# Rows of the expert weights w1 and w3 laid two to a partition, in a one-layer decoder kernel on Trainium2

## The chip, the cores and the metric

The kernel runs on one core of a Trainium2 chip. The metric is the device time of one execution in microseconds. Three runs of the kernel before took 893.99, 894.02 and 895.39 us; their median is 894.02 us.

## What is computed

One layer of a decoder: two token mixers, a cross-attention and a mixture of experts, each with a residual and a layer norm. The change touches the experts alone. There are 512 tokens of 1024 values and 16 experts; each token goes to two of them.

```
for e in range(N_EXPERTS):
    hidden = jax.nn.silu(hf @ w1[e]) * (hf @ w3[e])
    y = y + combine[:, e:e + 1] * (hidden @ w2[e])
```

w1[e] and w3[e] are 1024 x 512 in float32 (2 MB each), w2[e] is 512 x 1024 (2 MB). All 16 experts together are 96 MB, read from HBM once.

## The kernel before

The mixers and the cross-attention run first, up to about 594 us. The experts follow in a pipeline over e = 0 to 15, written out by hand.

**Weights.** The class `Weights` holds one list of all weight pieces of the program, each of 512 KB, in the order of their use. `load` issues one DMA on the SyncE queue (SPq in the profile, line 54) whenever a buffer is free. A buffer comes back when `done` is called for its piece, after the last matmul on it. The buffers are named raws, ring, ringout, xres, sbk and s; there are some forty of them in the expert stage. The order of the expert pieces is: eight of w1 and w3 of expert e (w1 and w3 in turn, `q_up[e]`), then four of w2 of expert e - 1 (`q_w2[e - 1]`). A piece of w1 or w3 is 256 rows of 512 values. Partition p of the buffer holds rows p and 128 + p of the piece, so each partition receives two runs of 2 KB from two places. A piece of w2 is 128 rows of 1024 values: partition p holds row p, one run of 4 KB.

A load waits for two things (its rows of the order below name them): for PE, which must be done with the buffer, and for one of eight counters DMAHW0 to DMAHW7. The counters are used in turn, so a load waits until the load eight places ahead of it has landed, and at most eight loads are on their way.

**Tokens.** Tokens of an expert are gathered from DRAM by `gather` (POOL, line 1158) into `ringgb` or `wx`, one token in a partition. `turn_in` (lines 1390 to 1397) turns them with eight TensorE transposes of 128 columns (line 1395) into `xgT[:, e % 2, c]`, c = 0 to 7: 128 of the 1024 values in the partitions, the tokens in the columns. In a transpose the tokens are the operand that is loaded as weights, and the identity is streamed.

**Expert.** `up(e)` multiplies chunk c of the turned tokens with chunk c of w1 and w3 (line 1422; the parts for more than 64 and more than 96 tokens, line 1433, are skipped by a branch, line 1409 or 1411, where the expert has fewer). So the values that sit in partition p of `xgT[:, c]` must belong to the weight row that sits in partition p of chunk c. Then `turn_in(e + 1)`, `gather(e + 3)`, `down(e - 1)` with w2 (lines 1463 and 1471), `to_rows` (ACT line 1486 and 1492, DVE line 1494), and `scatter` (POOL, line 1270), which adds the result rows to `yd` in DRAM.

**The end.** After the loop `last_loads` (lines 1524 to 1540) reads `yd` back with four loads of 512 KB on SPq (line 1530). They stand on SPq behind all weight loads, behind the end of a block that is built by `tc.If(n > 0)` (line 1264; the block itself is not executed), and they need the scatter of expert 13 and all earlier ones. ACT and DVE split the rows read (lines 190 and 191). Behind those splits in the order of the two engines stand the copies of the last expert's turned hidden values (lines 1586 and 1588), and PE's last w2 matmuls (line 1595) wait for those copies.

Line 495, in an earlier stage, matters as a comparison. Its streamed operand is read with this pattern, m being 1, 2, 4, 8, 16, 32 and 64 in turn:

```
qt = strided(Q[:, h, 2 * c * P:], n * g + m, [[P - m, 2], [2 * m, n // (2 * m)], [1, m]])
```

With m = 1 (the group I-776 of the profile) these are two runs of 16 columns, every second one; with m = 16 (I-1162) two runs of 16 neighbouring columns.

Of the kernel before, what the change touches and what calls it, by code (L numbers as in the profile page):

```python
# [16 lines left out]
P = 128  # L17
# [79 lines left out]
def tile_kernel(ctx, tc, x, mem, ln_in_g, ln_in_b, w_in, hg_lb_logits, hg_norm_g, w_branch_a, w_branch_b,  # L97
                w_mix_out, ln1_g, ln1_b, xa_wq, xa_wk, xa_wv, xa_wo, ln2_g, ln2_b,
                router_wg, router_bg, router_we, router_be, moe_w1, moe_w3, moe_w2, ln3_g, ln3_b, out):
    nc = tc.nc  # L100
# [8 lines left out]
    W = Weights(nc, 2)  # L109

    def block(w, c0, nk):

        return [W.add(w[2 * q * P:(2 * q + 2) * P, c0:c0 + 512].rearrange("(k p) n -> p k n", p=P))
                for q in range(nk // 2)]
# [9 lines left out]
    q_v.append(block(xa_wv, 512, 8))  # L124
    q_wo = [block(xa_wo, c, 8) for c in (0, 512)]

    q_up, q_w2 = {}, {}
    for e in range(17):
        if e < 16:
            q_up[e] = [tuple(W.add(w[0, e, 2 * q * P:(2 * q + 2) * P].rearrange("(k p) n -> p k n", p=P), True)  # L130
                             for w in (moe_w1, moe_w3)) for q in range(4)]
        if e > 0:
            q_w2[e - 1] = [W.add(moe_w2[0, e - 1, k * P:(k + 1) * P].rearrange("(k p) n -> p k n", p=P), True)
                           for k in range(4)]
# [5 lines left out]
    def msp():  # L140
        return ps.tile([P, 512], F32, tag="ms", name=nc.get_next_instruction_name() + "_ms")
# [34 lines left out]
    ident = pp.tile([P, P], F32, name="ident")  # L176
# [225 lines left out]
    for lv in range(5):  # L402
        n = 32 >> lv
# [36 lines left out]
    for lv in range(1, 8):  # L440
        n = 2048 >> lv
# [768 lines left out]
    t = NT - 1  # L1210
# [176 lines left out]
    gx = [wx.rearrange("p a n -> p (a n)"), gbr[:, 1]]  # L1387
    scratch = []

    def turn_in(e):  # L1390
        xg = gx[e % 2]
        for q in range(2):
            p = msp()
            for i in range(4):
                nc.tensor.transpose(p[:, i * P:(i + 1) * P], xg[:, (4 * q + i) * P:(4 * q + i + 1) * P], ident)  # L1395
            (nc.scalar.copy, nc.vector.tensor_copy)[q](xgT[:, e % 2, 4 * q:4 * q + 4],
                                                       p.rearrange("p (k n) -> p k n", n=P))

# [98 lines left out]
    for e in range(NE - 1):  # L1497
        h = up(e)
        turn_in(e + 1)
        if e + 3 < NE:  # L1500
            gather(e + 3)
        if e == 13:
            scratch.extend(W.raw_free.pop() for i in range(4))
            more_blocks()
            W.buffers(scratch)
        if e == 0:
            begin(tell_gates())
        if e > 0:
            for step in down(e - 1):
                step()  # L1510
            finish()
            scatter(to_rows(e - 1), gidx[:, e - 1:e])
        turn_hidden(e, h)
# [68 lines left out]
    p = msp()  # L1582
# [109 lines left out]
```

## Time and profile before

| What | Value |
|---|---|
| Median of three runs | 894.02 us |
| Profiled execution: its own time | 894.34 us |
| Span of the profile (first to last instruction) | 892.4 us |
| Mean granted TensorE clock | 0.989 of full speed |
| PE busy | 845.3 us, 95% of the span |
| DVE, ACT, POOL busy | 51%, 38%, 14% |
| SyncE queue (q1) | 157.31 MB in 71504 packets |
| All DMA | 177.65 MB, mean 199 GB/s |

The profiled execution is 0.32 us above the median of the three runs, and its span leaves out 1.94 us of its own time. Times of the rows below count from the start of the span. A line number of the profile is a line of the kernel above. "PEld" is the load of the operand that stays in TensorE, which overlaps the matmuls; "PEq" and "SPq" are the sequencers of PE and SyncE. In a row of the timeline the part in brackets is how long the engine was idle before it, and what ended that.

### The profile page before, as it was taken

What the parts mean: (1) busy time and instruction counts of PE and PEld (TensorE: products, weight loads), DVE (VectorE), ACT (ScalarE), POOL (GpSimd) and SP (SyncE); (2) the same over time, 40 slices, a digit from 0 to 9 for tenths busy, and PEclk for the clock granted to TensorE, in tenths of its full rate; (3) what the DMA queues carried; (4) which work ended last, traced back from release to release, by engine and by line L of the source; (5) the groups of instructions that cost most, each with busy time, mean ns of one, the idle gap of its engine ahead of it and who ended that gap; (6) DMA issues with size and microseconds to landing.
All of it is one profiled execution on the core that took longest, in us unless ns stands there. A gap on an engine that the chain in (4) does not pass through costs nothing. (4 is left out here: it accounts for less than half of the span.)

```text
span 892.4 us, 13680 instructions
## 1 busy us (share of the span) xinstructions
PE 845.3 (95%) x5296; PEld 582.1 (65%) x5296; DVE 458.6 (51%) x804; ACT 337.4 (38%) x640; POOL 128.4 (14%) x214
## 2 busy tenths in 40 slices
PE   7999999999999999999999999997999999799984
PEld 5888777788777777888988888763333333244343
DVE  6632576643757656759734667673423233223236
ACT  3332335643554544303624443222323233222234
POOL 5300000000312220005100000220211112110102
PEclk8999999999999999999999999999999999999998
DMA  8533323213222245422841766799999999999942
GB/s 298 174 98 95 95 73 94 71 49 95 71 71 72 71 139 177 140 88 80 239 158 48 235 214 236 250 372 343 390 353 356 333 343 339 342 366 360 370 170 94
DMA packets 79267, 177.65 MB, mean 199 GB/s; under 512 B 7797, under 2 KB 7829, under 8 KB 79184
## 3 DMA queue, kind: packets, MB, share of 16 engines
q1 hardware_dynamic: 71504, 157.31, 50.5%
q0 software_dynamic: 7536, 18.65, 6.7%
q8 instruction: 60, 0.98, 0.4%
q10 hardware_dynamic: 144, 0.52, 0.1%
q14 instruction: 23, 0.19, 0.1%
HBM read 168.47 MB, written 15.73 MB: 206 GB/s over the span
## 5 line engine op out<-in xcount | busy, mean ns | idle before, releaser
L1494 DVE TENSOR_SCALAR ringgb<-I-5389_acc,wgb 32x256 f32<-32x256 f32 x60 | 29.2, 487 | 122.5 <-ACT ringgb L1492 111.1
L1422 PE MATMUL I-5383_acc<-ring,xgT 128*64 128x512 f32 x284 | 77.9, 596 | 2.9 <-DMA ring<-in_moe_w_dram 2.9
L1486 ACT ACTIVATE ringgb<-I-5387_acc,wgb 64x512 f32<-64x512 f32 x30 | 20.5, 683 | 83.5 <-DMA yd<-ringgb,s 56.0
L67 DVE TENSOR_TENSOR I-69_out<-raws,I-69_out 128x1024 fp32r<-128x1024 f32 x24 | 29.3, 1223 | 38.2 <-ACT I-69_out L65 37.9
L1422 PEld LDWEIGHTS I-5383_acc<-ring,xgT 128*64 128x64 f32 x284 | 23.2, 137 | 36.9 <-issue 31.2
L1270 POOL DMA_INDIRECT yd<-ringgb,s x14 | 22.4, 1597 | 169.5 <-DVE I-8217w2k L1452 18.0
L660 DVE TENSOR_TENSOR_SCAN wx<-sbk 128x128 f32<-128x128 f32 (+3 forms) x32 | 27.1, 847 | 28.7 <-POOL sbk L656 28.7
L65 ACT CAST I-73_out<-raws 128x1024 fp32r<-128x1024 f32 x23 | 24.1, 1050 | 45.5 <-PE I-3563_acc L187 17.1
L67 DVE TENSOR_TENSOR I-71_out<-raws,I-71_out 128x1024 fp32r<-128x1024 f32 x22 | 26.9, 1223 | 24.6 <-ACT I-71_out L65 24.6
L65 ACT CAST I-69_out<-raws 128x1024 fp32r<-128x1024 f32 x25 | 26.2, 1050 | 32.6 <-issue 9.2
L65 ACT CAST I-71_out<-raws 128x1024 fp32r<-128x1024 f32 x24 | 25.3, 1055 | 24.9 <-PE I-384_acc L186 4.6
L67 DVE TENSOR_TENSOR I-73_out<-raws,I-73_out 128x1024 fp32r<-128x1024 f32 x21 | 25.7, 1222 | 16.1 <-ACT I-73_out L65 15.8
L1422 PE MATMUL I-5383_acc<-raws,xgT 128*64 128x512 f32 x64 | 30.0, 602 | 0.6 <-DMA raws<-in_moe_w_dram 0.6
L1492 ACT ACTIVATE ringgb<-I-5389_acc,wgb 32x256 f32<-32x256 f32 x60 | 27.8, 464 | 4.3 <-issue 2.2
L656 POOL TENSOR_SCALAR_AFFINE_SELECT sbk<-sbk 128x128 f32<-128x128 f32 x32 | 14.3, 447 | 94.5 <-ACT sbk L651 50.2
L1433 PE MATMUL I-5385_acc<-ring,xgT 128*32 128x256 f32 x408 | 26.4, 380 | 0.0
L1433 PEld LDWEIGHTS I-5385_acc<-ring,xgT 128*32 128x32 f32 x408 | 14.1, 110 | 13.8 <-issue 4.9
L213 POOL TENSOR_TENSOR I-1461hgss<-I-1461hgss,mhalf 128x4 f32<-128x4 f32 x1 | 1.0, 1047 | 136.4 <-DVE I-1461hgss L564 136.4
L1422 PE MATMUL I-5383_acc<-ringout,xgT 128*64 128x512 f32 x80 | 17.9, 595 | 0.0
L937 POOL MEMSET I-4802w2k<- 128x128 f32 x1 | 0.2, 204 | 110.0 <-PE I-4748_ms L187 110.0
L1422 PEld LDWEIGHTS I-5383_acc<-raws,xgT 128*64 128x64 f32 x64 | 8.1, 138 | 8.6 <-issue 7.0
L1158 POOL DMA_INDIRECT ringgb<-x2d,s x8 | 8.4, 1048 | 29.0 <-PE I-7818_ms L1395 9.8
(3489 smaller groups left out, 2397.3 us busy)
## 6 DMA issues: line engine op xcount, KB each, us to landing
ring<-in_moe_w_dram SPq DMA_DIRECT2D x114, 512.0 KB
raws<-in_w_in_dram SPq DMA_DIRECT2D x44, 512.0 KB
ringout<-in_moe_w_dram SPq DMA_DIRECT2D x32, 512.0 KB
raws<-in_moe_w_dram SPq DMA_DIRECT2D x20, 512.0 KB
xres<-in_moe_w_dram SPq DMA_DIRECT2D x16, 512.0 KB
raws<-in_xa_wk_dram SPq DMA_DIRECT2D x7, 512.0 KB
raws<-in_xa_wv_dram SPq DMA_DIRECT2D x7, 512.0 KB
raws<-in_w_mix_out_dram SPq DMA_DIRECT2D x6, 512.0 KB
```

Of the source, the lines that this page charges most:

```text
L65: self.nc.scalar.copy(hi, raw)
L67: eng.tensor_tensor(lo, raw, hi.bitcast(F32), op=ALU.subtract)
L213: nc.gpsimd.tensor_tensor(o, v, mhalf[:, :v.shape[-1]], op=ALU.pow)
L656: nc.gpsimd.affine_select(kp[:, d], kp[:, d], pattern=[[-1, P]], compare_op=ALU.is_gt, fill=1.0, base=w * (P - 1), channel_multiplier=1 - ...
L660: nc.vector.tensor_tensor_scan(rest[:, :n][:, ::-1], kp[:, n:0:-1], kp[:, n:0:-1], 1.0, ALU.mult, ALU.bypass)
L1158: nc.gpsimd.indirect_dma_start(out=gx[e % 2], out_offset=None, in_=x2d[:, :], in_offset=bass.IndirectOffsetOnAxis(ap=gidx[:, e:e + 1], axi ...
L1270: nc.gpsimd.indirect_dma_start(out=yd[:, :], out_offset=bass.IndirectOffsetOnAxis(ap=idx, axis=0), in_=y, in_offset=None, bounds_check=T - ...
L1422: nc.tensor.matmul(a[64 * i:64 * i + 64], x[:, c, 0:64], w[:, k * 512:(k + 1) * 512], start=c == 0, stop=c == 7)
L1433: nc.tensor.matmul(b[32 * i:32 * i + 32, 256 * g:256 * g + 256], x[:, c, 64 + 32 * g:96 + 32 * g], ws[c // 2][i // 2][:, o:o + 256], start ...
L1486: nc.scalar.activation(y[0:64, n * 512:(n + 1) * 512], a[s], AF.Copy, scale=gates_at[s, 0, e:e + 1])
L1492: nc.scalar.activation(o, z, AF.Copy, scale=f)
L1494: nc.vector.tensor_scalar(o, z, f, None, op0=ALU.mult)
```

## The change

Two places change. The pieces of w1 and w3 of experts 1 to 15 are read so that partition p of the buffer holds rows 2p and 2p + 1 of the piece: one run of 4 KB, as in w2. Expert 0 keeps its layout, because its tokens come another way (they are gathered by matmuls, not by `turn_in`). And `turn_in` takes, for chunk c = 2q + k, every second column of the 256 columns of piece q, from column k on, so that tokens and weight rows fit again. The buffers, the matmuls of `up`, the copies out of PSUM and the number of bytes stay as they are.

```
-            q_up[e] = [tuple(W.add(w[0, e, 2 * q * P:(2 * q + 2) * P].rearrange("(k p) n -> p k n", p=P), True)
+            q_up[e] = [tuple(W.add(w[0, e, 2 * q * P:(2 * q + 2) * P].rearrange("(k p) n -> p k n", p=P) if e == 0 else
+                                   w[0, e, 2 * q * P:(2 * q + 2) * P].rearrange("(p k) n -> p (k n)", k=2)[:, None], True)
                              for w in (moe_w1, moe_w3)) for q in range(4)]
...
     def turn_in(e):
-        xg = gx[e % 2]
+        xg = gx[e % 2].rearrange("t (q p k) -> t q k p", q=4, k=2)
         for q in range(2):
             p = msp()
             for i in range(4):
-                nc.tensor.transpose(p[:, i * P:(i + 1) * P], xg[:, (4 * q + i) * P:(4 * q + i + 1) * P], ident)
+                nc.tensor.transpose(p[:, i * P:(i + 1) * P], xg[:, 2 * q + i // 2, i % 2], ident)
```

No instruction moves on any engine and none is added or removed; after the first place, line numbers are three higher. On SPq, at the last four of expert 15's loads of w1 and w3 and the first three of expert 14's loads of w2 (the buffer stands left of the arrow), the order before is:

```order
L54 DMA ring4_4376<-in_moe_w1_dram 128x2x512 [waits DMAHW7_49,PE_49]
L54 DMA ring11_4717<-in_moe_w3_dram 128x2x512 [waits DMAHW0_49,PE_49]
L54 DMA ring11_4717<-in_moe_w1_dram 128x2x512 [waits DMAHW1_49,PE_49]
L54 DMA ring12_4720<-in_moe_w3_dram 128x2x512 [waits DMAHW2_49,PE_49]
L54 DMA ring12_4720<-in_moe_w2_dram 128x1024 [waits DMAHW3_49,PE_49]
L54 DMA ring6_4723<-in_moe_w2_dram 128x1024 [waits DMAHW4_49,PE_49]
L54 DMA ring6_4723<-in_moe_w2_dram 128x1024 [waits DMAHW5_49,PE_49]
```

and with the change:

```order
L54 DMA ring4_4376<-in_moe_w1_dram 128x1024 [waits DMAHW7_49,PE_49]
L54 DMA ring11_4717<-in_moe_w3_dram 128x1024 [waits DMAHW0_49,PE_49]
L54 DMA ring11_4717<-in_moe_w1_dram 128x1024 [waits DMAHW1_49,PE_49]
L54 DMA ring12_4720<-in_moe_w3_dram 128x1024 [waits DMAHW2_49,PE_49]
L54 DMA ring12_4720<-in_moe_w2_dram 128x1024 [waits DMAHW3_49,PE_49]
L54 DMA ring6_4723<-in_moe_w2_dram 128x1024 [waits DMAHW4_49,PE_49]
L54 DMA ring6_4723<-in_moe_w2_dram 128x1024 [waits DMAHW5_49,PE_49]
```

The loads of w1 and w3 have the shape of the w2 loads now; buffers, places and waits are the same. On PE, at the end of expert 2's `up` and at `turn_in(3)` (tokens in ringgb), the order before is:

```order
L1433 MATMUL I-5385_acc<-ring_5044,xgT 32x256 x8
L1411 UNCONDITIONAL_BRANCH x2
L1409 UNCONDITIONAL_BRANCH
L1395 MATMUL I-5911_ms<-ident,ringgb 128x128 x4
L1395 MATMUL I-5918_ms<-ident,ringgb 128x128 x4
L1463 MATMUL I-5387_acc<-ring_5138,I-5803w2k 64x512 x4
```

and with the change:

```order
L1436 MATMUL I-5385_acc<-ring_5044,xgT 32x256 x8
L1414 UNCONDITIONAL_BRANCH x2
L1412 UNCONDITIONAL_BRANCH
L1398 MATMUL I-5911_ms<-ident,ringgb 128x128 x4
L1398 MATMUL I-5918_ms<-ident,ringgb 128x128 x4
L1466 MATMUL I-5387_acc<-ring_5138,I-5803w2k 64x512 x4
```

Only the line numbers differ; that the transposes read every second column does not show in such a row.

## Rows read from the trace of the kernel before

**Rows 1.** The page, part 2: tenths busy in 40 slices of 22.3 us.

```profile
PE   7999999999999999999999999997999999799984
...
DMA  8533323213222245422841766799999999999942
```

**Rows 2.** By stretch: PE, PEld, DVE, ACT, POOL busy, PEclk, DMA share, GB/s.

```profile
760.00:780.00 20.00, 13.35 (x55) 4.76 (x52) 4.70 (x8) 5.55 (x10) 2.64 (x2) 0.91 0.98 351
842.50:846.00 3.50, 3.50 (x20) 1.22 (x18) 1.97 (x4) 0.00 (x0) 1.41 (x2) 1.00 1.02 407
846.00:850.00 4.00, 4.00 (x54) 1.75 (x53) 1.56 (x3) 0.59 (x1) 0.74 (x2) 1.00 0.67 204
640.00:840.00 200.00, 182.68 (x1342) 73.29 (x1338) 56.44 (x96) 59.56 (x108) 29.62 (x22) 0.99 0.99 353
```

**Rows 3.** Waits of PE, 755 to 790 us: total, times, longest.

```profile
PE I-5383_acc L1422 <- DMA ring<-in_moe_w_dram: 2.9, 3, 1.5
PE I-5383_acc L1422 <- DMA s<-in_moe_w_dram: 0.7, 1, 0.7
PE I-5383_acc L1422 <- DMA raws<-in_moe_w_dram: 0.6, 1, 0.6
```

**Rows 4.** Timeline of PE, two groups of line L1463: start, length.

```profile
692.57 3.65 PE L1463 MATMUL I-5387_acc<-ringout,I-6563w2k 128*64 128x512 f32 x16
...
774.38 4.97 PE L1463 MATMUL I-5387_acc<-ring,I-7513w2k 128*64 128x512 f32 x15 [3.14 <-issue]
```

**Rows 5.** Timeline of the DMA queue SPq, 800 to 862 us.

```profile
807.49 0.60 SPq L54 DMA_DIRECT2D ring<-in_moe_w_dram  x1
808.77 4.34 SPq L54 DMA_DIRECT2D raws<-in_moe_w_dram  x2
...
839.72 0.33 SPq L54 DMA_DIRECT2D s<-in_moe_w_dram  x1
841.05 1.65 SPq L54 DMA_DIRECT2D ring<-in_moe_w_dram  x2
855.57 1.77 SPq L1530 DMA_DIRECT2D ringout<-yd  x4
```

**Rows 6.** Line L1264, SPq: ns of one, first and last start.

```profile
L1264 SPq EVENT_SEMAPHORE  x9: 17/17/17, 844.1 to 855.2; - x9
```

**Rows 7.** The chain that ended last, in order of time.

```profile
856.06 4.44 DMA ringout<-yd
...
861.66 1.24 DVE zp L191
```

**Rows 8.** Timeline of all engines, 838 to 866 us.

```profile
844.59 1.56 POOL L1270 DMA_INDIRECT yd<-ringgb,s  x1 [16.79 <-DVE I-8392w2k L1452]
...
858.89 1.93 PE L1471 MATMUL I-5389_acc<-ring,I-8392w2k 128*32 128x256 f32 x32
...
863.70 1.12 PE L1595 MATMUL I-5383_acc<-ring,I-8529w2k 128*128 128x512 f32 x2 [2.87 <-ACT I-8529w2k L1588]
```

**Rows 9.** DMA issues, scatter of results: count, median us to landing.

```profile
yd<-ringgb,s POOLq DMA_INDIRECT x14, 9.0
```

**Rows 10.** DMA queue, 522 to 535 us, runs of 2 KB: packets, MB, share.

```profile
q1 hardware_dynamic: 2169, 4.18, 88.6%
```

**Rows 11.** DMA queue, 842.5 to 846 us, runs of 4 KB.

```profile
q1 hardware_dynamic: 391, 1.43, 101.8%
```

**Rows 12.** DMA queue, 640 to 840 us, both kinds.

```profile
q1 hardware_dynamic: 27954, 64.14, 86.4%
```

**Rows 13.** Line L1395, four weight loads: min/median/max ns, first and last start.

```profile
L1395 PEld LDWEIGHTS I-5685_ms<-ident,wx x4: 137/140/143, 617.0 to 617.3; 128*128 128x128 f32 x4
```

**Rows 14.** Line L495, m = 1 (I-776) and m = 16 (I-1162).

```profile
L495 PE MATMUL I-776_ms<-hgQ,wx x64: 191/196/218, 99.4 to 101.6; 128*32 128x32 f32 x64
...
L495 PE MATMUL I-1162_ms<-hgQ,wx x64: 196/196/217, 137.3 to 139.6; 128*32 128x32 f32 x64
```

**Rows 15.** Timeline of PE, the wait for the first gathered tokens.

```profile
606.74 1.11 PE L1395 MATMUL I-5542_ms<-ident,ringgb 128*128 128x128 f32 x4 [4.00 <-DMA ringgb<-x2d,s]
```

## Prediction

> **What bounds the kernel now.** I read the page's slices first. PE is at 9 tenths in nearly every slice, and from about 580 us on the DMA engines are at 9 tenths too, until about 850 us [rows 1]. So the expert stage is the one place where bytes can be the limit, and the change touches only that stage. Over 640 to 840 us the DMA share is 0.99 at 353 GB/s, while PE has a matmul in flight for 182.7 of 200 us [rows 2]. Two engines that are both nearly full say little on which one is waited for, so I went to the waits.
>
> PE starves in one stretch. Between 755 and 790 us its waits for pieces of w1 and w3 are 2.9, 0.7 and 0.6 us, together 4.2 us [rows 3]. In the same stretch the granted clock is 0.91 [rows 2], and one group of 15 matmuls of line 1463 takes 4.97 us, where 16 took 3.65 us at the full clock [rows 4]. That is 4.97 - 15/16 x 3.65 = 1.5 us lost at the lower level (1.2 GHz) after those idle times. The 3.14 us before that group [rows 4] have no releaser in the profile; I leave them where they are.
>
> The second place is the end. The chain that ended last starts on SPq: the first reads of yd are issued at 855.57 us [rows 5], they take 4.44 us, and the split of the rows read and the two copies behind it follow [rows 7]. PE's last w2 matmuls start at 863.70 us after 2.87 us of idle time for those copies [rows 8]; PE had been done at 858.89 + 1.93 = 860.82 us. Why does SPq issue at 855.57 and not earlier? Its last weight load was issued soon after 841.05 us [rows 5]. Then it stands at line 1264 and goes through nine waits, the first at 844.1, the last at 855.2 us [rows 6]. Nothing of PE is waited for there. These are the eight DMA counters, that is, the landing of the last weight loads. In 846 to 850 us the DMA share is only 0.67 [rows 2]: some of the 16 engines are still draining their part while others are done. So **the end of the kernel hangs on the end of the weight stream**, and PE only has to be there in time.
>
> **What the change removes.** Each load of w1 or w3 becomes 128 runs of 4 KB instead of 256 of 2 KB; per DMA engine 8 packets instead of 16. What is that worth? The trace has both kinds.
> - In 522 to 535 us the queue carries only w1 and w3: 0.886 x 16 x 13 us = 184.3 us for 4.18 MB / 2048 = 2041 packets, 90 ns each [rows 10].
> - In 842.5 to 846 us it carries only w2: 1.018 x 16 x 3.5 us = 57.0 us for 1.43 MB / 4096 = 349 packets, 163 ns each [rows 11].
> - So one load costs an engine 16 x 90.3 = 1.445 us in the one form and 8 x 163.3 = 1.307 us in the other: 0.14 us less.
> - Over 640 to 840 us both kinds are mixed, two thirds of the bytes in 2 KB runs by the order of the list: 2764.8 us for 20879 and 5220 packets [rows 12]. With 90.3 ns for the small ones, 168 ns are left for a large one, and the difference is 1.445 - 1.348 = 0.10 us a load.
> - The strictest row is the pace of SPq near the end. A load is issued when the one eight places ahead has landed. The loads at 807.49 and 808.77 us follow the landing of two w2 loads, 1.28 us apart; those at 839.72 and 841.05 us follow two loads of expert 15's w1 and w3, 1.33 us apart [rows 5]. That is 0.05 us a load.
>
> The ends are 0.05 and 0.14 us. I take 0.07 us, nearer to the pace, because the pace is set by the engine that lands last, and that engine also sets the end.
>
> How many loads count? The first forty or so only need the buffers to be there, and their successors wait for PE, which begins at about 594 us. I count experts 5 to 15: 88 loads; from expert 6 it is 80, from 4 it is 96. The weight stream then ends 88 x 0.07 = **6.2 us** earlier.
>
> **What that moves.** At the end, the nine waits of line 1264 end at 855.2 - 6.2 = 849.0 us. What is late next? The reads of yd also need the scatter of expert 13: issued at 844.59 us [rows 8], 9.0 us to landing by the median [rows 9], so 853.6 us, 1.6 us before the weights. It moves only as far as PE and the two engines behind it move. By expert 12, 64 loads have given 64 x 0.07 = 4.5 us, which is enough for the 4.2 us of waits; with those gone the 1.5 us at the lower clock may go too, but the loads don't allow more than 4.5. So the scatter lands at about 849.1 us, and SPq is free 6.1 us earlier. PE is done at 860.8 - 4.5 = 856.3 us and could be called from 863.7 - 6.1 = 857.6 us on, so it still waits there for 1.3 us. Behind that the program is the same. The sum is a gain of 6.1 us.
>
> **What it adds.** No instruction. The 120 transposes of `turn_in` (8 for each of experts 1 to 15) load their weights from every second column. One group of four starts its weight loads within 617.0 to 617.3 us, 140 ns each, about 0.11 us apart [rows 13]. No row shows a weight load with a step. The nearest rows are streamed operands: 64 matmuls with every second column take a median of 196 ns, and with neighbouring columns 196 ns too [rows 14]. So I take nothing, with a bound of nothing below (it reads no fewer columns) and a doubling above, 8 x 0.11 = 0.9 us an expert, which the first rival prices. The Trainium skill's page "SBUF — State Buffer" (section "Door 1: The DMA port swizzle") says that an engine reading with a step keeps its full rate while at least two accesses fall into one 16-byte line; two float32 of four do here. No run here shows it for weight loads.
>
> The gathers share the DMA engines with the weights. PE waits 4.00 us for the first gathered tokens [rows 15]. An engine has eight rows of a gather; if each lets one weight packet pass, which is now 163 instead of 90 ns, the wait grows by 0.6 us. PE's 1.3 us at the end hide it from PE, but the scatter of expert 13 moves by it. I take nothing and keep 0.6 us as the bound.
>
> **The rivals.**
> - **Slower: the stepped weight loads cost.** At a doubling PE has 15 x 0.88 = 13.2 us more to do, on its own path in the experts where the weights are there in time. It has 4.2 + 1.5 + 2.9 = 8.6 us of idle and slow time to pay with, so the kernel loses 4.6 us: **898.6 us**. It decides from 8.6 us / 120 = 72 ns a transpose on. For it: there is no such load in the trace. Against it: [rows 14].
> - **No change: the bytes bind, not the packets.** Then loads of either form take the same time beside each other, and the time stays at **894.0 us**. For it: the pace differs by only 0.05 us, and at 353 GB/s [rows 2] the memory itself could be the limit. Against it: 407 GB/s with 4 KB packets alone [rows 2]. The Trainium skill's page "DMA: Bandwidth & Descriptors" (section Specifications) speaks for this rival: runs of 512 B already reach the line rate, and one core's share of HBM is about 358 GB/s. By that rule the gain is nothing. The stretch at 407 GB/s is above that share.
> - **Half of it:** the stream ends earlier, but the scatter of expert 13 or a gather does not follow, because PE gains little. A scatter that moves by 1.5 us only lets SPq go 3.1 us earlier: **890.9 us**.
> - **More:** with 0.10 us and more a load the stream no longer binds; PE's 8.6 us and the 3.1 us without a releaser go too: **about 883 us**.
>
> **How the numbers follow.** The profiled execution took 894.34 us, 0.32 above the median of the runs. 894.3 - 6.1 = 888.2 us, and 0.3 less against the median: 887.9 us. The forecast's own range runs from 80 x 0.05 = 4.0 us (890.0) to the 8.6 us that PE can give up (885.4). A measurement of this kernel can tell about 0.2%, 1.8 us, from no change. Chances: the forecast 0.53, half of it 0.09, more 0.06, no change 0.18, slower 0.14. Faster is 0.53 + 0.09 + 0.06 = 0.68. For 8 in 10 the range leaves out the slower rival (0.14) and the lower part of "more" (0.03): 884.5 to 895.0 us.
>
> **What would show it.** In the profile after: the queue's packets fall by 15 x 8 x 128 = 15360; the waits for w1 and w3 at 755 to 790 us are gone or under 1 us, and the clock there stays at 1.00; the last wait of line 1264 on SPq is at about 849 us; the transposes still take 140 ns. Wrong would be: longer weight loads at line 1398 (the slower rival), or waits of SPq that end where they did (no change), or an end of line 1264 that moved while the reads of yd wait for the scatter (half).

## The result, and the profile after

The changed kernel takes **889.95 us** (median of 8 runs, 887.37 to 893.52). The kernel before took 895.04 us beside it (8 runs, 893.99 to 896.91). The medians differ by 5.1 us; the ratio of the comparison is 0.9924, with a 95% interval of 0.9903 to 0.9944, which is 0.56 to 0.97% faster. In a later comparison, on one chip, it was 890.23 against 896.13 us, 0.9937 (0.9914 to 0.9960). The medians thus differ by 5.1 and 5.9 us, and the two intervals together allow 4 to 9 us; 6.1 had been forecast, from 894.02 us. From the 895.04 us of this comparison the same 6.1 would have given 888.9.

The changed kernel's profiled run took 890.44 us, its span is 888.3 us. The packets of SPq's queue fell from 71504 to 56144, by 15360:

```profile
q1 hardware_dynamic: 56144, 157.31, 49.4%
```

The page's slices, 22.2 us each, answer [rows 1]: the rows look much the same, so the change hardly shows at this distance.

```profile
PE   6999999999999999999999999998989999889994
...
DMA  8433232223212225331852567599999999999942
```

The stretches (PE, PEld, DVE, ACT, POOL busy, PEclk, DMA share, GB/s) answer [rows 2]:

```profile
760.00:780.00 20.00, 17.26 (x82) 6.63 (x80) 4.70 (x8) 5.58 (x10) 2.64 (x2) 1.00 1.00 362
840.00:846.00 6.00, 6.00 (x32) 1.82 (x32) 3.52 (x7) 0.30 (x1) 2.15 (x2) 1.00 0.74 267
846.00:850.00 4.00, 4.00 (x76) 2.40 (x80) 0.68 (x1) 0.59 (x1) 0.00 (x0) 1.00 0.36 77
640.00:840.00 200.00, 185.22 (x1358) 76.45 (x1354) 56.42 (x96) 62.66 (x114) 29.61 (x22) 1.00 0.99 360
```

Over 640 to 840 us the DMA engines are as full as before, 0.99, but they move 360 GB/s instead of 353. PE is busy for 2.5 us more of the 200. At 760 to 780 us the granted clock is 1.00, the upper level, where it was 0.91. Between 755 and 790 us PE still waits for two pieces of w1 and w3, 2.3 us in place of 4.2 [rows 3]:

```profile
PE I-5383_acc L1425 <- DMA ring<-in_moe_w_dram: 1.8, 1, 1.8
PE I-5383_acc L1425 <- DMA s<-in_moe_w_dram: 0.5, 1, 0.5
```

The timeline of PE has the group of line 1466 that answers the slow one of [rows 4]. It takes 3.65 us, as the other group of [rows 4] did, and the idle time without a releaser ahead of it is 1.59 us instead of 3.14:

```profile
772.47 3.65 PE L1466 MATMUL I-5387_acc<-ring,I-7513w2k 128*64 128x512 f32 x15 [1.59 <-issue]
```

The end, in the order of [rows 5] to [rows 8]. First SPq's last loads and the reads of yd (timeline: start, length):

```profile
806.10 1.61 SPq L54 DMA_DIRECT2D raws<-in_moe_w_dram  x2
...
837.50 1.60 SPq L54 DMA_DIRECT2D ring<-in_moe_w_dram  x2
851.41 1.78 SPq L1533 DMA_DIRECT2D ringout<-yd  x4
```

The nine waits of line 1267 (ns of one, first and last start):

```profile
L1267 SPq EVENT_SEMAPHORE  x9: 17/17/17, 840.5 to 851.0; - x9
```

The first pieces of the chain that ended last (start, length):

```profile
859.19 0.43 issue
859.61 3.67 PE I-5383_acc L1598 x8
```

And the timeline of PE's last groups, with the copy on ACT that the last one needs:

```profile
857.12 1.93 PE L1474 MATMUL I-5389_acc<-ring,I-8392w2k 128*32 128x256 f32 x32
858.82 0.27 ACT L1591 COPY I-8529w2k<-I-8523_ms 128x128 f32<-128x128 f32 x1 [1.75 <-DVE I-8529w2k L1589]
859.61 1.10 PE L1598 MATMUL I-5383_acc<-ring,I-8529w2k 128*128 128x512 f32 x2 [0.56 <-PEq L1414]
```

Here the change is plain. The last loads are issued from 837.50 us on instead of 841.05. The nine waits end at 851.0 us instead of 855.2, the reads of yd go out at 851.41 instead of 855.57. And the chain no longer begins at SPq: behind line 1474 (done at 857.12 + 1.93 = 859.05 us) PE stands for 0.56 us for its own sequencer, where it waited 2.87 us for the split rows before [rows 8]. The copy is done at 858.82 + 0.27 = 859.09 us, so PE and the chain from SPq now end within 0.1 us of each other, and what is left is PE's own. In a second profile of the changed kernel the copy is done 1.1 us ahead of PE.

**A ruler for the experiments.** The expert stage does not start at one time: its first matmul of w1 stands at 594.9 us before and at 596.2 after, though nothing ahead of it was changed, and in a second profile of the changed kernel at 598.0. This row of the changed kernel shows the start (after the durations in ns: first and last start):

```profile
L1425 PE MATMUL I-5383_acc<-ring,xgT x284: 592/592/1116, 596.2 to 845.4; 128*64 128x512 f32 x142
```

So I count from that matmul to two later points, from one profiled run of each kernel: the first read of yd, and the start of the last w2 matmuls (line 1595, after: 1598).

| kernel | stage starts, us | reads of yd, us later | last w2 matmuls, us later | ratio of times (95%) |
|---|---|---|---|---|
| before | 594.9 | 260.7 | 268.8 | |
| after | 596.2 | 255.2 | 263.4 | 0.9924 (0.9903 to 0.9944) |
| after, second time | 598.0 | 253.6 | 263.3 | 0.9937 (0.9914 to 0.9960) |
| transposes alone | 596.1 | 260.4 | 268.5 | 0.9998 (0.9983 to 1.0012) |
| loads alone | 594.6 | 254.8 | 263.0 | 0.9936 (0.9914 to 0.9958) |
| experts 1 to 7 | 596.6 | 258.4 | 266.5 | 0.9971 (0.9953 to 0.9989) |
| experts 8 to 15 | 596.5 | 257.8 | 265.9 | 0.9948 (0.9933 to 0.9963) |
| runs of 1 KB | 595.3 | 272.8 | 284.2 | 1.0152 (1.0117 to 1.0188) |
| every 4th column | 596.6 | 253.6 | 263.4 | 0.9925 (0.9898 to 0.9953) |
| every 8th column | 596.0 | 254.4 | 262.5 | 0.9930 (0.9903 to 0.9958) |
| before without `more_blocks` | 595.1 | 257.9 | 267.9 | 0.9998 (0.9983 to 1.0012) |
| after without `more_blocks` | 597.5 | 254.4 | 264.1 | 0.9936 (0.9913 to 0.9958) |
| columns ordered ahead | 598.9 | 252.2 | 260.4 | 0.9935 (0.9914 to 0.9956) |

By this ruler the change shortens the stage by 268.8 - 263.4 = **5.4 us**. The two profiles of the changed kernel agree within 0.1 us at the last w2 matmuls, but only within 1.6 us at the reads of yd.

### The profile page after: what moved, and what is told of

It reads as the page before. It is cut to its first block, busy times and chain, and to the rows that moved or that the text cites. A ratio compares the mean times of both kernels' runs of the same rounds, so it can differ in the third digit from the quotient of the medians.

```text
span 888.3 us, 13677 instructions
## 1 busy us (share of the span) xinstructions
PE 846.5 (95%) x5296; PEld 585.1 (66%) x5296; DVE 458.7 (52%) x804; ACT 337.2 (38%) x640; POOL 128.4 (14%) x214
## 3 DMA queue, kind: packets, MB, share of 16 engines
q1 hardware_dynamic: 56144, 157.31, 49.4%
## 5 line engine op out<-in xcount | busy, mean ns | idle before, releaser
L1425 PEld LDWEIGHTS I-5383_acc<-ringout,xgT 128*64 128x64 f32 x80 | 5.6, 137 | 10.6 <-issue 10.6
```

Of the source, the lines that this page charges most:

```text
L1425: nc.tensor.matmul(a[64 * i:64 * i + 64], x[:, c, 0:64], w[:, k * 512:(k + 1) * 512], start=c == 0, stop=c == 7)
```

## The experiments

### The two halves of the change, each alone

Transposes alone, against the changed kernel:

```diff
-            q_up[e] = [tuple(W.add(w[0, e, 2 * q * P:(2 * q + 2) * P].rearrange("(k p) n -> p k n", p=P) if e == 0 else
+            q_up[e] = [tuple(W.add(w[0, e, 2 * q * P:(2 * q + 2) * P].rearrange("(k p) n -> p k n", p=P) if e < 16 else
```

> The tokens of experts 1 to 15 are transposed from every second column, the loads keep their 2 KB runs (the tokens' columns then do not fit the rows of w1 and w3: the result is another, the work is the same). In the trace of the changed kernel a group of four such transposes takes about 0.71 us of PE where it took 0.63, so 30 groups are 2.4 us more. Theory (the weight stream sets the end, the step costs PE 2.4 us): the stream is as before and PE has idle time, so the time is the kernel before plus 0 to 2.4 us, about 895 us, and the last wait of line 1264 on SPq stays at 855 to 857 us. Rival (the step costs PE a doubling, 13 us): about 898.6 us. Rival (the step is free): as before, 894 us, and weight loads of 140 ns.

Loads alone, against the changed kernel:

```diff
-        xg = gx[e % 2].rearrange("t (q p k) -> t q k p", q=4, k=2)
+        xg = gx[e % 2]
...
-                nc.tensor.transpose(p[:, i * P:(i + 1) * P], xg[:, 2 * q + i // 2, i % 2], ident)
+                nc.tensor.transpose(p[:, i * P:(i + 1) * P], xg[:, (4 * q + i) * P:(4 * q + i + 1) * P], ident)
```

> The loads of w1 and w3 of experts 1 to 15 have 4 KB runs, the tokens are transposed from neighbouring columns (they then do not fit the rows of the weights: the result is another, the work is the same). Theory (the stream ends earlier, and behind that PE sets the end): PE gets back up to 2.4 us against the changed kernel, so 887.6 to 890.0 us, with weight loads of 140 ns and the queue's packets at 56144. Rival (the weight stream still sets the end after the change, PE's 2.4 us are hidden): the same as the changed kernel, 890 us. Rival (bytes bind, and the gain seen came from something else than the loads): 894 us.

And the changed kernel beside them:

> The changed kernel beside the others on one chip: 890 us, a ratio of about 0.992 to 0.994 to the kernel before.

Measured: 895.89 us for the transposes alone, 890.26 us for the loads alone, 890.23 us for both, 896.13 us before. **The loads make the whole gain; the transposes change nothing that the time shows.** Yet the stepped weight loads do cost PE something. The transposes' line, in the kernel with the transposes alone and in that with the loads alone (min/median/max ns, first and last start):

```profile
L1398 PEld LDWEIGHTS I-5685_ms<-ident,wx x4: 196/208/216, 618.3 to 618.6; 128*128 128x128 f32 x4
```

```profile
L1398 PEld LDWEIGHTS I-5685_ms<-ident,wx x4: 138/141/143, 616.1 to 616.4; 128*128 128x128 f32 x4
```

208 ns with the step, 141 without, and 140 in [rows 13]. What that is worth on PE stands in its timeline, from a group of four transposes to the first matmul behind the second group; the kernel before, then the changed one:

```profile
617.03 0.63 PE L1395 MATMUL I-5685_ms<-ident,wx 128*128 128x128 f32 x4 [0.31 <-PEq L1409]
617.50 0.60 PE L1395 MATMUL I-5692_ms<-ident,wx 128*128 128x128 f32 x4
618.02 0.65 PE L1463 MATMUL I-5387_acc<-ring,I-5565w2k 128*64 128x512 f32 x2
```

```profile
617.95 0.71 PE L1398 MATMUL I-5685_ms<-ident,wx 128*128 128x128 f32 x4 [0.31 <-PEq L1412]
618.50 0.65 PE L1398 MATMUL I-5692_ms<-ident,wx 128*128 128x128 f32 x4
619.07 0.65 PE L1466 MATMUL I-5387_acc<-ring,I-5565w2k 128*64 128x512 f32 x2
```

Eight transposes take 1.12 us instead of 0.99; for 15 experts that is 15 x 0.13 = 2.0 us. Who pays? PE's idle time ahead of the last w2 matmuls does. It was 2.87 us before [rows 8]. Here it is with the transposes alone, then with the loads alone:

```profile
PE I-5383_acc L1598 <- ACT I-8529w2k L1591: 2.5, 1, 2.5
```

```profile
PE I-5383_acc L1598 <- ACT I-8529w2k L1591: 1.5, 1, 1.5
```

With both it is 0.56 us, and no longer a wait for data. With the loads alone PE was done with line 1474 this early:

```profile
854.16 1.93 PE L1474 MATMUL I-5389_acc<-ring,I-8392w2k 128*32 128x256 f32 x32
```

That is 856.09 us, 261.5 us after the stage's start; with both it is 859.05 us, 262.9 us after it. So 1.4 of the step's 2.0 us reach PE's end, and they use up the 1.5 us that PE would have waited there. The last w2 matmuls start only 0.4 us later in the stage (263.4 against 263.0), which is less than the times can tell.

### Half of the experts

The condition on the expert number, in the loads and in `turn_in` (here for experts 8 to 15; the other has `e == 0 or e > 7`):

```diff
-            q_up[e] = [tuple(W.add(w[0, e, 2 * q * P:(2 * q + 2) * P].rearrange("(k p) n -> p k n", p=P) if e == 0 else
+            q_up[e] = [tuple(W.add(w[0, e, 2 * q * P:(2 * q + 2) * P].rearrange("(k p) n -> p k n", p=P) if e < 8 else
...
+        plain = e < 8
+        xg = gx[e % 2] if plain else gx[e % 2].rearrange("t (q p k) -> t q k p", q=4, k=2)
```

> Only experts 8 to 15 have the 4 KB runs and the stepped transposes: 64 of the 120 loads. Theory (each load in the stretch where the stream binds gives about 0.06 us): 64 x 0.06 = 3.8 us less stream, PE 1.3 us more, about 890 to 891.5 us. Rival (the gain is made at the waits of 755 to 790 us, by a lead that the stream has won in the experts before them): the loads of experts 8 to 12 alone give 40 x 0.06 = 2.4 us there, so the time is 892 us or more.

> Only experts 1 to 7 have the 4 KB runs and the stepped transposes: 56 of the 120 loads. With only experts 8 to 15 changed the kernel won 0.5% of the 0.64% that the whole change won. Theory (the stream binds from about expert 5 on, and each load in it gives 0.06 to 0.07 us): 16 to 24 loads count, 1.0 to 1.7 us of gain, a ratio of about 0.998 to 0.999; the two parts add up to the whole. Rival (the stream binds from the first expert on, through the landing of the loads ahead): 56 x 0.065 = 3.6 us, 0.996.

Measured: 892.0 us for experts 8 to 15 and 893.69 us for 1 to 7. In the stage they win 2.9 and 2.3 us, together 5.2 of the whole change's 5.4: the two halves add up. (In the times they win 4.1 and 3.1 us, each against the kernel before on its own chip; the intervals of the three ratios allow that sum too, and that of experts 1 to 7, 0.9953 to 0.9989, holds both expectations. Only the stage tells them apart.) Neither expectation of where the loads begin to count holds for experts 1 to 7. At the price of a load found below (0.059 us), 2.3 us is some 38 loads of the 56, not the 16 to 24 of the first theory and not all 56 as in the rival. In the late half, 2.9 us is 49 of 64 loads; why not all of them count there was not tried.

The bytes that SPq's queue moves show where the gain is made, in three stretches counted from the stage's start (MB; the last begins at about 790 us of the span):

| kernel | 0 to 80 us | 80 to 140 us | 195 to 245 us |
|---|---|---|---|
| before | 26.36 | 18.40 | 16.54 |
| transposes alone | 26.43 | 18.34 | 16.58 |
| experts 1 to 7 | 27.14 | 18.34 | 16.46 |
| experts 8 to 15 | 26.42 | 19.09 | 17.21 |
| loads alone | 27.18 | 19.17 | 17.07 |
| after | 26.91 | 19.00 | 17.37 |

Each half moves more bytes where its own loads run, and no more than the kernel before where they don't. So the stream gains all along the stage, behind 790 us too. That speaks against the rival that the gain is made at 755 to 790 us alone, which the times could not decide: it leaves experts 8 to 15 with 2.4 us, near the measured 2.9. The start of the gain shows as well: the 40th weight load of the experts, the last of expert 3's w1 and w3, is issued 4.8 us ahead of the stage before and 4.9 after. So the loads of experts 1 to 3 win nothing, and 32 of the 56 are left, fewer than the 38 by the price.

### Runs of 1 KB: the other direction

```diff
-            q_up[e] = [tuple(W.add(w[0, e, 2 * q * P:(2 * q + 2) * P].rearrange("(k p) n -> p k n", p=P), True)
+            q_up[e] = [tuple(W.add(w[0, e, 2 * q * P:(2 * q + 2) * P].rearrange("(k p) n -> p k n", p=P) if e == 0 else
+                                   w[0, e, 2 * q * P:(2 * q + 2) * P].rearrange("(k p) (h n) -> p h k n", p=P, h=2), True)
...
+            to = (buf.rearrange("p (h k n) -> p h k n", h=2, k=2) if len(ap.shape) == 4 else
+                  buf.rearrange("p (k n) -> p k n", n=ap.shape[-1]))
```

> The kernel before with w1 and w3 of experts 1 to 15 in runs of 1 KB, each row in two halves that lie apart in the buffer (the columns then come to the multiplication in another order: the result is another, the work is the same). Packets of the queue: 71504 + 30720 = 102224. Theory (each packet costs an engine a fixed time beside its bytes; from the medians of 84 ns for 2 KB and 159 ns for 4 KB that is 9 ns): a 1 KB packet takes about 47 ns, a load 32 x 47 = 1.49 us against 1.34, 0.14 us more, and the 88 to 120 loads make the kernel 12 to 17 us slower, about 907 to 912 us. Rival (bytes bind): 894 to 896 us and the stream ends where it did. Rival (the fixed time is the 17 ns that 90 and 163 ns give): 0.27 us a load, 24 to 33 us slower.

Measured: 911.18 us, 1.52% or 14.4 us slower, inside the 12 to 17 us of the theory. This run decides against "bytes bind": the bytes are the same. It can't tell a packet's own cost from that of reading shorter pieces of the weights in HBM, since both change together here, as they do in the change itself. The queue over 640 to 840 us (packets, MB, share of the 16 engines' time), first of this kernel, then of the changed one; that of before is [rows 12]:

```profile
q1 hardware_dynamic: 45580, 60.52, 87.8%
```

```profile
q1 hardware_dynamic: 18014, 65.59, 85.9%
```

One number falls out of each row, the time that a load of 512 KB (0.5243 MB) takes of the 16 engines. Before: 64.14 / 0.5243 = 122.3 loads in 0.864 x 200 = 172.8 us, 1.412 us a load. After: 125.1 loads in 171.8 us, 1.373 us. With 1 KB: 115.4 loads in 175.6 us, 1.521 us. Two thirds of the loads are of w1 and w3, so one of these wins 0.039 x 3/2 = **0.059 us** from 2 to 4 KB, and loses 0.109 x 3/2 = 0.163 us from 2 to 1 KB. In the records of the single packets the medians are 46, 84 and 159 ns for 1, 2 and 4 KB: 75 ns for each 2 KB and about 9 ns for the packet itself.

By them a load of w1 or w3 wins 16 x 84 - 8 x 159 = 72 ns, or 0.072 us.

The stage grew by 284.2 - 268.8 = 15.4 us. Not all of that is the stream. SPq's nine waits, and then the reads of yd in the chain that ended last:

```profile
L1267 SPq EVENT_SEMAPHORE  x9: 17/17/17, 856.7 to 867.8; - x9
```

```profile
868.64 7.68 DMA ringout<-yd
```

The nine waits end 867.8 - 595.3 = 272.5 us after the stage's start, where they ended at 260.3: the stream is 12.2 us longer, 12.2 / 0.163 = 75 loads. The other 3.2 us are the reads of yd, which take 7.68 us instead of 4.44 although the weights have landed; why is open. With the change the nine waits end at 254.8, 5.5 us earlier, or 93 loads; in its second profile (849.5 us) at 251.5, 8.8 us earlier, more than all 120 loads would give. The two doses have the right signs and about the right sizes, but they don't fix one count of loads. PE waits for the split rows behind the reads of yd, longer than in any other kernel:

```profile
PE I-5383_acc L1598 <- ACT I-8529w2k L1591: 6.9, 1, 6.9
```

### A larger step

```diff
-        xg = gx[e % 2].rearrange("t (q p k) -> t q k p", q=4, k=2)
+        xg = gx[e % 2].rearrange("t (q p k) -> t q k p", q=2, k=4)
...
-                nc.tensor.transpose(p[:, i * P:(i + 1) * P], xg[:, 2 * q + i // 2, i % 2], ident)
+                nc.tensor.transpose(p[:, i * P:(i + 1) * P], xg[:, q, i], ident)
```

For every eighth column the tokens are taken as `"t (p k) -> t k p"` with k = 8.

> The changed kernel with the tokens transposed from every fourth column (they then do not fit the rows of the weights: the result is another, the work is the same). A weight load took 140 ns with neighbouring columns and 208 ns with every second. Theory (the time goes by the 16-byte lines that are touched): every fourth column touches four times as many, 140 + 3 x 68 = 344 ns, and eight transposes take about 0.13 x 3 = 0.4 us more than in the kernel before; PE has hardly any idle time left at the end, so the kernel is some 4 us slower than the changed one, 894 us. Rival (any step costs the same): 208 ns and 890 us.

> The same with every eighth column. Theory (16-byte lines): no more lines than with every fourth column, so 344 ns and the time of that kernel. Rival (the time goes by the stretch of memory between the first and the last column): 140 + 7 x 68 = 616 ns, and over 1 us more for eight transposes: 15 us and more. Rival (any step costs the same): 208 ns and 890 us.

Measured: 890.40 and 890.04 us, and these weight loads, with every fourth and then with every eighth column:

```profile
L1398 PEld LDWEIGHTS I-5685_ms<-ident,wx x4: 196/209/218, 616.6 to 616.9; 128*128 128x128 f32 x4
```

```profile
L1398 PEld LDWEIGHTS I-5685_ms<-ident,wx x4: 185/193/207, 617.7 to 618.0; 128*128 128x128 f32 x4
```

The theory of 16-byte lines fell: 209 and 193 ns, not 344. A step of 2, 4 or 8 columns costs about the same; the price is for having a step at all, 53 to 69 ns a load. What makes it is open.

### Taking SPq's waits away

The branch that this input does not take is left out, in the kernel before and in the changed one:

```diff
         if e == 13:
             scratch.extend(W.raw_free.pop() for i in range(4))
-            more_blocks()
             W.buffers(scratch)
```

> The kernel before without the call of more_blocks (line 1264), whose branch this input does not take: the path for experts with more than 128 tokens is left out, and with it the nine waits of SPq for the last weight loads. Theory (the end of the weight stream sets the end through these waits): the reads of yd wait for the scatter of expert 13 alone, go out 1 to 2 us earlier against the start of the experts, and the last w2 matmuls start as much earlier; in the kernel before they start 268.8 us after the first matmul of expert 0's w1, here at 266.8 to 268.0; the time is 892 to 893 us, a ratio of 0.998. Rival (SPq's wait is not what the end waits for): 268.8 us and 894 us.

> The changed kernel without the call of more_blocks. Theory (there PE itself sets the end: its last w2 matmuls wait for nothing but 0.4 to 0.6 us): the reads of yd may go earlier, but the last w2 matmuls start where they did, 263.3 to 263.4 us after the first matmul of expert 0's w1; 890 us. Rival (the end of the stream still sets it): 1 us or more earlier, like the kernel before without the call.

Measured: 895.43 us (before: 895.56) and 890.22 us. The times say "nothing", the traces say more. The chain of the kernel before without the branch (start, length):

```profile
843.87 8.92 DMA yd<-ringgb,s
852.93 0.33 SPq L1529
853.36 6.44 DMA ringout<-yd
...
862.99 5.10 PE I-5383_acc L1594 x8
```

Its stretch of 863 to 866 us (columns as above):

```profile
863.00:866.00 3.00, 3.00 (x4) 1.42 (x5) 0.26 (x1) 2.87 (x6) 0.00 (x0) 0.53 0.21 85
```

As expected, the reads of yd are now released by the scatter of expert 13, and go out 2.8 us earlier in the stage. But they take 6.44 us instead of 4.44 [rows 7]. The likely cause is that the last weights are still under way on the same 16 engines; that the reads can also be slow behind landed weights was seen with the runs of 1 KB. Of 2.8 us, 0.9 is left at the last w2 matmuls, and these run at the lower clock level (1.2 GHz; granted 0.53), behind 2.82 us without a matmul. Their first half takes 5.10 us, where it takes 3.67 in the changed kernel (its chain, above), and nothing is left. The changed kernel without the branch behaves in the same way. Its reads take 6.13 us, and the last w2 matmuls, expected where they were, start 0.7 us later in the stage; their first half takes 5.40 us there. Its chain, and then PE's wait ahead of these matmuls:

```profile
842.92 8.82 DMA yd<-ringgb,s
851.89 0.33 SPq L1533
852.31 6.13 DMA ringout<-yd
```

```profile
PE I-5383_acc L1598 <- ACT I-8378w2k L1591: 2.5, 1, 2.5
```

So the nine waits on SPq are how the end of the stream reaches the end of the kernel, but they are not its cost. Without them the reads go out earlier, take longer and end nearly where they did.

### Columns ordered ahead of the experts

All 16 experts have 4 KB runs, the transposes have no step. The second normalisation writes the tokens in the order of the weights' rows:

```diff
+    def normalise_paired(xt, mv, gb):
+        for h in (slice(0, T), slice(T, D)):
+            tmp = work("w2k", [P, T], bufs=5)
+            two = lambda x: x.rearrange("p (q j k) -> p q k j", q=2, k=2)
+            nc.vector.scalar_tensor_tensor(tmp, xt[:, h], mv[:, 0:1], gb[0][:, h], op0=ALU.subtract, op1=ALU.mult)
+            for k in range(2):
+                nc.vector.scalar_tensor_tensor(xt[:, h].rearrange("p (q k j) -> p q k j", q=2, k=2)[:, :, k],
+                                               two(tmp)[:, :, k], mv[:, 3:4], two(gb[1][:, h])[:, :, k],
+                                               op0=ALU.mult, op1=ALU.add)
```

> A version with the 4 KB runs for all 16 experts and no stepped transposes: the second normalisation writes the tokens with their columns already in the order of the rows of w1 and w3 (in halves, six instructions of DVE a tile instead of two), and what reads them later (the gathers, expert 0's tokens, the start of yd) follows. Theory (PE sets the end of the changed kernel): PE does 2.0 us less, the stream is 8 loads of 0.06 us shorter, so the last w2 matmuls start 262 to 263 us after the first matmul of expert 0's w1 instead of 263.3; the four tiles' normalisation costs DVE some 0.3 us each, of which the last tile's lies ahead of the experts: 888.5 to 890.5 us. Rival (the stream and the scatter of expert 13 set the end as much as PE, as where the transposes were not stepped): 263.0 us and 890 us or, with the longer normalisation, 891 us.

Measured: 889.89 us, 0.9935: not told apart from the changed kernel. The stage is 3.0 us shorter than the changed kernel's (260.4 against 263.4), more than expected. But it starts later: the 31st weight load of the experts, which is issued 14.9 us ahead of the first matmul in every other kernel, is issued 16.3 us ahead of it here. That is 1.4 us; the longer normalisation of the last tile, which stands ahead of the experts and had been estimated at 0.3 us, is the likely cause, but no run shows it alone. What remains is 1.6 us, 0.2%, which this comparison can't tell from nothing. In its stage the scatter of expert 13 is what ends last:

```profile
842.36 8.56 DMA yd<-ringgb,s
851.07 0.34 SPq L1546
851.57 4.47 DMA ringout<-yd
```

## Why the prediction was right, and where it was not

The forecast was 887.9 us with 884.5 to 895.0 around it; 889.95 was measured.

- **The price of a load was right.** 0.07 us was taken from between 0.05 and 0.14; the shares of the stage give 0.059, the medians of the packets 0.072. The pace of SPq was the right row to lean on, and the two isolated stretches of [rows 10] and [rows 11] overstated it.
- **The count of 88 is not tested to the load.** By the end of the stream it is 93 with the change (and more in its second profile) and 75 with runs of 1 KB. That loads count only from expert 5 on was too late: experts 1 to 7 alone bring some 38 loads' worth, where experts 5 to 7 have 24, and the queue's issues begin to differ behind expert 3.
- **The stream's end** was to move by 6.2 us. Against the start of the stage the nine waits end 260.3 us later before and 254.8 us later after: 5.5 us; in the second profile of the changed kernel it is 8.8 us, so one profile does not size this term. Their absolute time, 851.0 and not 849.0 us, also holds the 1.3 us by which this stage starts later.
- **The waits at 755 to 790 us** were to vanish or fall under 1 us. They fell to 2.3 us, so this was mis-sized. That PE also arrives earlier when its weights do is a likely reason, but not shown. The clock of 1.00 there was right.
- **The transposes at nothing: wrong.** The loads take 208 ns, not 140, and 2.0 us of PE come with them. The step of the prediction that failed is to take the streamed operand of [rows 14] for the loaded one. The bound (0.9 us an expert) held: it is 0.13. The total was saved by a cover that the sum had not planned for this, and that is luck: the 1.3 us that PE was to wait at the end are gone, since 1.4 of the 2.0 us reached PE's end. PE was to be done 4.5 us earlier; it is so with the loads alone (4.4 us in the stage) and 3.0 us earlier with both. The 0.56 us left are its own sequencer's, so the next thing of this kind would be paid in full. The Trainium skill's page "SBUF — State Buffer" (section "Door 1: The DMA port swizzle") has full rate for two accesses in one 16-byte line. The trace differs for weight loads: two of four float32 in a line take 208 ns against 140, and one in a line takes 209, no more.
- **What is late next** was named rightly: the scatter of expert 13. In the second profile of the changed kernel it is what releases the reads of yd, while the weights were there 2 us earlier:

```profile
844.46 7.03 DMA yd<-ringgb,s
851.64 0.34 SPq L1533
```

- **The end hangs on the stream**: right, but not by the queue's order alone, as the runs without `more_blocks` show.
- **The size of the gain.** By the ruler 5.4 us against 6.1. In the terms of the sum, 88 x 0.059 = 5.2 us of stream where 88 x 0.07 gave 6.2; at the end it is PE, with the transposes, that sets the 5.4.
- **The rivals.** "Slower" needed 72 ns a transpose; the step costs 0.13 us / 8 = 16 ns. "The bytes bind" is refuted by the runs of 1 KB. The rule on which it leaned, the Trainium skill's page "DMA: Bandwidth & Descriptors" (section Specifications), lets runs of 512 B reach the line rate; here 640 to 840 us moved 332, 353 and 360 GB/s with w1 and w3 in 1, 2 and 4 KB runs. The row with 1 KB:

```profile
DMA packets 48641, 66.48 MB, mean 332 GB/s; under 512 B 3522, under 2 KB 42143, under 8 KB 48613
```

 "Half" gave 890.9 us, and the measured 889.95 lies nearer to it (0.95 us) than to the forecast (2.05 us). Taken from the 895.04 us of the same comparison, the two would be 891.9 and 888.9, and the forecast is nearer. The mechanism of "half" did not run: the reads of yd moved by 5.5 us in the stage, not by 3.1. "More" did not come: a load wins less than 0.10 us, and in the second profile, where the stream ends 8.8 us earlier, the last w2 matmuls start only 5.5 us earlier, with PE ending last.

## What to carry to other kernels

Where the DMA engines are full, count packets and not only bytes: here each packet costs about 9 ns beside its bytes, and 15360 packets fewer shortened a stage of 260 us by 5.4 us. Price the change at the pace of the queue in the very stretch that binds, and test it with a dose in the other direction, which is larger and easier to measure; read the dose where the stream ends, as what stands behind it can change too. A cost that a change adds off the path may vanish only because the same change has left idle time elsewhere; name that idle time and see how much of it is left.

## What the runs showed of the hardware that was not expected

- A weight load of 128 x 128 float32 takes 140 ns from neighbouring columns, 208 ns from every second, 209 from every fourth, 193 from every eighth; four loads one after the other then stand 0.14 us apart instead of 0.12. A streamed operand with every second column took 196 ns either way [rows 14].
- Reads of 512 KB from DRAM that start before the last weights have landed take 6.1 to 6.4 us instead of 4.4. They took 7.68 us with runs of 1 KB, where the weights had landed.
- Behind 2.82 us without a matmul the granted clock was 0.53 in 863 to 866 us of the kernel before without `more_blocks`; behind 2.87 us at nearly the same place in the kernel before it stayed at 1.00 (863.7 to 866.7 us). With experts 1 to 7 alone it fell too, behind only 2.09 us (0.65 in 863.14 to 868 us; the first half of the last w2 matmuls took 5.40 us there). The length of the idle time alone does not tell which.
